# Sliding-window attention in slots: scores ahead of outputs and transposed probabilities, outputs a slot later, three probability buffers

## Chip, cores and metric

The kernel runs on one core of one Trainium2 chip. The metric is the device time of one execution in microseconds (us). The engines are named as in the profile: PE is the TensorE matrix engine, PEld its weight loads, DVE the VectorE, ACT the ScalarE, SP the engine that issues the DMAs here.

## The reference

The block has 1024 positions of width 1024. One input projection gives the operands of two branches: a gated linear attention (branch A) and sliding-window attention (branch B). Their gated sum goes through an output projection, and then a SwiGLU layer follows. Only branch B's attention is touched. Its heads: eight query heads of 128, two key/value heads (groups g = 0, 1, four query heads each). What it computes, for one query block of 128 positions and the up to three key blocks around it:

```
q, k = rms_norm(q) * q_g, rms_norm(k) * k_g        # then rotary positions
s = (q @ k^T) / sqrt(128), outside +-128: masked
p = softmax over [s, sink logit of the head]       # the sink has no value
o = p @ v
```

## The kernel before, in words

All matrices are float32, split in a high and a low half (names ending in h and l), and a product is three matmuls (`mm3`: high by high, high by low, low by high).

The section runs 16 tiles, numbered n = 8 g + t for group g and query block t, in 22 slots. In a slot, `slot` calls a list of stages; behind each stage it gives an equal share of the slot's n dense matmuls, the **fills** (`fill`): 128x512 matmuls of the projection of branch A's output gate, which depend on nothing in the attention. A slot has 26 fills for the first two slots, 15 up to slot 18 and 18 afterwards. So PE has fills to do between the stages, but runs all in the order in which the program writes it (`manual_schedule`): when a stage's matmul waits, the fills behind it wait. The order on DVE, ACT and SP is chosen when the program is built, by when operands are expected; each engine runs its list in that order.

The stages of tile n (in brackets the slot before the change):

- `k_load` and `a_load` (n - 1, n): DMA loads of value (kvr), key and query rows (qr).
- `k_prep` (n): value halves vSh (ACT), vSl (DVE). `a_prep` (n + 1): square on ACT (into sq4), sum on DVE (L867), normalising factor rs, and rotary products on DVE (L912, L914, L916, L917, result qn).
- `k_turn` (n + 1): keys transposed on PE (L900) into a `ch` tile, copied in halves to kTh, kTl. `a_turn` (n + 2): four query heads transposed (L923), copied to sqh (ACT L926) and sql (DVE L927).
- `a_scores` (n + 3), one stage per head: `mm3` into a `ch` tile, its mask addition and maximum in one DVE instruction (L941, writes p and mx). After the fourth head: mx, nm, es on DVE (L948 to L952), four exponentials on ACT with their sums (L956), dn and rd on DVE (L958, L960), four scalings of p on ACT (L962).
- `a_probs` (n + 5), one stage per key block: p transposed for four heads (L973) into a `ch` tile, copied to ph (ACT L976) and pl (DVE L977).
- `a_out` (n + 5): up to nine matmuls of ph, pl with vSh, vSl into a `ch` tile, a copy sob (ACT L987), four DMAs (L989).

All `ch` tiles come from one pool (psc, line 38) of four PSUM tiles, so a stage that wants a new one waits until the last reader of a tile's earlier content has run. Four more PSUM tiles (psm) belong to the fills; their results leave through DVE (L125) and a `stg` tile to DRAM. Weights of the fills are split on ACT (L70, wh) and DVE (L72, wl).

Within a slot the stages are sorted by the tuple `order`. The slots' contents are in the table `todo`. At t = 19 the pool of the small left-side tiles is closed, and `prep_b(0)` starts loading attention outputs back (lo, L1009), each split in obh (ACT L1001) and obl (DVE L1002), for the projection `branch_b(0)`, which follows the last slot and the remaining fills. Loads into lo have two buffers; their memory is that of pools that were just closed.

Of the kernel before, what the change touches and what calls it, by code (L numbers as in the profile page):

```python
# [8 lines left out]
F32 = mybir.dt.float32  # L9
# [5 lines left out]
P = 128  # L15
# [15 lines left out]
def body(tc, i, out):  # L31
    nc = tc.nc
    with ExitStack() as root:
# [8 lines left out]
        def nm(s):  # L42
            uid[0] += 1
            return f"{s}_{uid[0]}"
# [4 lines left out]
        def chtile(shape, dt=F32):  # L49
            return psc.tile(list(shape), dt, tag="ch", name=nm("ch"))  # L50
# [27 lines left out]
        def mm3(o, ah, al, bh, bl, start, stop):  # L78
            mm(o, ah, bh, start, False)
            mm(o, ah, bl, False, False)  # L80
            mm(o, al, bh, False, stop)
# [26 lines left out]
        stgs = ExitStack()  # L108
# [502 lines left out]
        stg = glas.enter_context(tc.tile_pool(name="stgA", bufs=4))  # L611
# [208 lines left out]
        with tc.manual_schedule(engines={mybir.EngineType.PE}):  # L820
            fill(24)
            for t in range(last + 1):
                n = 24 if t < 2 else 16 if t < 4 else 12 if t < NH * NC + 4 else 8 if t < last - 1 else 18
# [9 lines left out]

        sc_ = swas.enter_context(tc.tile_pool(name="swc", bufs=1))
        swe = swas.enter_context(tc.tile_pool(name="swe", bufs=2))
        stg = stgs.enter_context(tc.tile_pool(name="stg", bufs=4, side="right"))
        swl = stgs.enter_context(tc.tile_pool(name="swl", bufs=2, side="right"))
        swm = stgs.enter_context(tc.tile_pool(name="swm", bufs=1, side="right"))

        class sw:  # L840
            def tile(shape, dt, tag, name, bufs=2):
                pool = swm if tag in ("p", "ph", "pl") else swe if tag in (
                    "kvr", "key", "sq4", "qn4", "qr", "qh", "ql") else swl
                return pool.tile(shape, dt, tag=tag, name=name, bufs=bufs)
        cosb = load_const(sc_, "cosb", i["c_cos"], (P, KT, 64))
        sinb = load_const(sc_, "sinb", i["c_sin"], (P, KT, 64))
# [17 lines left out]
        def inv_norm(raw, n, sq, scale, epsv, eps_t):  # L864
            ss = sw.tile([P, n], F32, tag=f"ss{n}", name=nm("ss"))
            nc.scalar.activation(sq, raw[:, 0:n], AF.Square)
            nc.vector.tensor_reduce(ss, sq, axis=mybir.AxisListType.X, op=ALU.add)  # L867
            rs = sw.tile([P, n], F32, tag=f"rs{n}", name=nm("rs"), bufs=4)
            rsqrt(rs, ss, scale, epsv, eps_t, sw, (P, n), f"sn{n}")
            return rs  # L870
# [9 lines left out]
        def k_load(t):  # L880
            raws[t] = sw.tile([P, 256], F32, tag="kvr", name=nm("kvr"))
            need(("skv", t))
            nc.sync.dma_start(out=raws[t], in_=scr["skv", t][:, 256:512])
            keys[t] = sw.tile([P, 2, P], F32, tag="key", name=nm("key"))
            nc.sync.dma_start(out=keys[t].rearrange("p a b -> p (a b)"), in_=scr["key", t])
# [19 lines left out]
        def a_prep(g, n):  # L905
            a = att[g, n] = Chunk()
            qr = raws.pop((g, n))

            b = sw.tile([P, 4, P], F32, tag="sq4", name=nm("sq"))
            a.rs = inv_norm(qr, 4, b, 1.0, EPS * 128, eps128)  # L910
            a.qn = sw.tile([P, 4, P], F32, tag="qn4", name=nm("qn"))
            nc.vector.tensor_tensor(b[:, :, 0:64], qr[:, :, 64:128], qB[:, n:n + 1, 0:64].to_broadcast([P, 4, 64]),  # L912
                                    op=ALU.mult)
            nc.vector.tensor_tensor(b[:, :, 64:128], qr[:, :, 0:64], qB[:, n:n + 1, 64:128].to_broadcast([P, 4, 64]),  # L914
                                    op=ALU.mult)
            nc.vector.tensor_tensor(a.qn, qr, qA[:, n:n + 1].to_broadcast([P, 4, P]), op=ALU.mult)  # L916
            nc.vector.tensor_tensor(a.qn, a.qn, b, op=ALU.add)  # L917
# [13 lines left out]
        def a_scores(g, n, h):  # L931
            a = att[g, n]
            if h == 0:
                a.p = sw.tile([P, 4, 384], F32, tag="p", name=nm("p"))
                a.mx = sw.tile([P, 4], F32, tag="mx", name=nm("mx"))
            w, p, mx = a.w, a.p, a.mx
            ks = slice(a.b0 * P, (a.b1 + 1) * P)
            mo = (a.b0 - (n - 1)) * P
            s = chtile((P, 384))
            mm3(s[:, :w], a.qh[:, h], a.ql[:, h], kTh[:, g, ks], kTl[:, g, ks], True, True)  # L940
            nc.vector.tensor_tensor_reduce(out=p[:, h, :w], in0=s[:, :w], in1=band[:, mo:mo + w],  # L941
                                           op0=ALU.add, op1=ALU.max, scale=1.0, scalar=-1e30,
                                           accum_out=mx[:, h:h + 1])
            if h < 3:
                return
            sk = sink[:, 4 * g:4 * g + 4]
            nm_ = sw.tile([P, 4], F32, tag="nm", name=nm("nm"))
            nc.vector.tensor_tensor(mx, mx, a.rs, op=ALU.mult)  # L948
            nc.vector.tensor_tensor(mx, mx, sk, op=ALU.max)
            nc.vector.tensor_scalar(nm_, mx, -1.0, None, op0=ALU.mult)  # L950
            es = sw.tile([P, 4], F32, tag="es", name=nm("es"))
            nc.vector.tensor_tensor(es, sk, mx, op=ALU.subtract)  # L952
            nc.scalar.activation(es, es, AF.Exp)
            dn = sw.tile([P, 4], F32, tag="dn", name=nm("dn"))
            for h in range(4):
                nc.scalar.activation(p[:, h, :w], p[:, h, :w], AF.Exp, bias=nm_[:, h:h + 1],  # L956
                                     scale=a.rs[:, h:h + 1], accum_out=dn[:, h:h + 1])
            nc.vector.tensor_tensor(dn, dn, es, op=ALU.add)  # L958
            rd = sw.tile([P, 4], F32, tag="rd", name=nm("rd"))
            nc.vector.reciprocal(rd, dn)  # L960
            for h in range(4):
                nc.scalar.activation(p[:, h, :w], p[:, h, :w], AF.Copy, scale=rd[:, h:h + 1])  # L962
# [32 lines left out]
        oa, ob, mh, ml = {}, {}, {}, {}  # L995
# [16 lines left out]
        todo = [[] for _ in range(2 * KT + 6)]  # L1012
        for n in range(2 * KT):
            g, t = divmod(n, KT)
            todo[n + 5].append((a_out, g, t))
            todo[n + 5] += [(a_probs, g, t, kb) for kb in range(3)]
            todo[n + 3] += [(a_scores, g, t, h) for h in range(4)]
            todo[n + 2].append((a_turn, g, t))
            todo[n + 1].append((a_prep, g, t))
            if n < KT:  # L1020
                todo[n + 1].append((k_turn, n))
                todo[n].append((k_prep, n))
                if n:
                    todo[n - 1].append((k_load, n))
            todo[n].append((a_load, g, t))
        order = (a_probs, k_prep, a_prep, a_scores, a_turn, k_turn, a_out, k_load, a_load)
        k_load(0)
        with tc.manual_schedule(engines={mybir.EngineType.PE}):
            for t, v in enumerate(todo):
# [507 lines left out]
```

## Time and profile before

| | us |
|---|---|
| median of 3 runs | 1649.15 (1649.06 to 1649.78) |
| profiled execution | 1649.93 |
| its span | 1648.1 |
| PE busy in the span | 1628.2 (99%) |
| DVE, ACT busy | 1249.4 (76%), 872.3 (53%) |
| the attention slots | about 566 to 745 |

The span runs from the first to the last recorded instruction; 1.8 us of the profiled execution lie around it. In rows of the profile, "out<-in" names tiles, "L941" is a line of the program, and a bracket such as [0.48 <-DVE mx L941] is idle time of the engine just before the row and what released it. Matmuls are pipelined: a row of 0.39 us can be followed by the next matmul 0.23 us after its start.

### The profile page before, as it was taken

How to read it: one execution, taken by the hardware profiler on the slowest of the kernel's cores; microseconds unless marked ns; L12 is line 12 of the kernel's file. 1: busy time of each engine (PE TensorE's matmuls, PEld its weight loads, DVE VectorE, ACT ScalarE, POOL GpSimd, SP SyncE). 2: the span in 40 equal slices, each digit the busy share in tenths (PEclk: the TensorE clock that was granted, in tenths of full speed). 3: DMA queues.
4: the chain of work that ended last, by engine and by line, in shares of the span. 5: the costliest groups of instructions: out<-in, count | busy, mean ns of one | idle time of the engine just before them, and what ended most of it. 6: DMA issues, size and time to landing. Idle time of an engine off the chain costs nothing.

```text
span 1648.1 us, 23225 instructions
## 1 busy us (share of the span) xinstructions
PE 1628.2 (99%) x7588; PEld 1346.5 (82%) x7588; DVE 1249.4 (76%) x2559; ACT 872.3 (53%) x1826; POOL 0.2 (0%) x4
## 2 busy tenths in 40 slices
PE   9999999999999999999999999999999999999999
PEld 7888888888888778878888888888888888888887
DVE  8867665589986599857885678887777778779655
ACT  8622224468998688885554557333333333354442
POOL 0000000000000000000000000000000000000000
PEclk9999999999999999999999999999999999999999
DMA  7554334485554633238765554453334443496433
GB/s 235 171 184 147 116 118 138 170 253 173 178 162 128 190 115 97 74 124 280 226 205 171 168 152 148 128 160 109 103 109 155 146 147 128 168 349 192 147 98 120
DMA packets 168010, 262.90 MB, mean 160 GB/s; under 512 B 19325, under 2 KB 52861, under 8 KB 167889
## 3 DMA queue, kind: packets, MB, share of 16 engines
q1 hardware_dynamic: 167888, 261.42, 49.9%
q8 instruction: 60, 0.98, 0.3%
q14 instruction: 62, 0.50, 0.1%
HBM read 187.93 MB, written 73.42 MB: 159 GB/s over the span
## 4 chain that ended last, share of the span: by engine, by line
PE 84%; DVE 8%; ACT 5%; DMA 1%; issue 1%; SPq 0%; ACTq 0%
PE mm L76 23%; PE mm L306 9%; PE mm L308 9%; PE mm L307 9%; PE mm L1350 7%; PE ch L1350 5%; PE ch L76 4%; PE ch L308 4%; PE ch L307 4%; PE ch L306 4%; PE ch L460 3%; PE mm L460 2%; ACT p L956 1%; DVE cs L655 1%; DVE wl L72 1%
## 5 line engine op out<-in xcount | busy, mean ns | idle before, releaser
L298 ACT ACTIVATE wh<-ws 128x512 fp32r<-128x512 f32 x132 | 83.3, 632 | 196.6 <-PE mm L307 104.5
L70 ACT ACTIVATE wh<-wr 128x512 fp32r<-128x512 f32 x202 | 124.9, 626 | 83.3 <-PE mm L76 47.7
L72 DVE TENSOR_TENSOR wl<-wr,wh 128x512 fp32r<-128x512 f32 x202 | 137.2, 684 | 26.3 <-ACT wh L70 26.1
L298 ACT ACTIVATE wh<-wr 128x512 fp32r<-128x512 f32 x69 | 43.6, 632 | 125.0 <-issue 49.9
L299 DVE TENSOR_TENSOR wl<-ws,wh 128x512 fp32r<-128x512 f32 x132 | 90.2, 684 | 22.4 <-ACT wh L298 22.3
L298 ACT ACTIVATE wh<-a 128x512 fp32r<-128x512 f32 x64 | 40.5, 633 | 91.1 <-PE mm L1350 42.6
L76 PE MATMUL mm<-wh,xl 128*128 128x512 f32 x192 | 83.0, 432 | 0.0
L76 PE MATMUL mm<-wh,xh 128*128 128x512 f32 x192 | 79.7, 415 | 0.0
L76 PE MATMUL mm<-wl,xh 128*128 128x512 f32 x192 | 79.6, 414 | 0.0
L299 DVE TENSOR_TENSOR wl<-a,wh 128x512 fp32r<-128x512 f32 x64 | 44.2, 690 | 43.0 <-ACT wh L298 42.6
L1350 PE MATMUL mm<-hh,wh 128*128 128x512 f32 x176 | 68.5, 389 | 0.0
L1350 PE MATMUL mm<-hl,wh 128*128 128x512 f32 x176 | 68.5, 389 | 0.0
L1350 PE MATMUL mm<-hh,wl 128*128 128x512 f32 x176 | 68.5, 389 | 0.0
L76 PE MATMUL mm<-xh,wh 128*128 128x512 f32 x160 | 64.6, 404 | 1.2 <-ACT wh L70 1.2
L76 PE MATMUL mm<-xl,wh 128*128 128x512 f32 x160 | 64.5, 403 | 0.1
L76 PE MATMUL mm<-xh,wl 128*128 128x512 f32 x160 | 59.2, 409 | 0.0
L1320 DVE TENSOR_TENSOR hl<-hr,hh 128x512 fp32r<-128x512 f32 x75 | 51.3, 684 | 3.7 <-ACT hh L1319 3.7
L1350 PE MATMUL ch<-hh,wh 128*128 128x512 f32 x132 | 51.3, 389 | 0.0
L1350 PE MATMUL ch<-hl,wh 128*128 128x512 f32 x132 | 51.3, 389 | 0.0
L1350 PE MATMUL ch<-hh,wl 128*128 128x512 f32 x132 | 51.3, 389 | 0.0
L76 PE MATMUL mm<-oah,wh 128*128 128x512 f32 x128 | 50.2, 392 | 0.0
L76 PE MATMUL mm<-oal,wh 128*128 128x512 f32 x128 | 49.8, 389 | 0.0
(620 smaller groups left out, 5058.6 us busy)
## 6 DMA issues: line engine op xcount, KB each, us to landing
wr<-in_w_fi_dram SPq DMA_DIRECT2D x102, 256.0 KB
wr<-in_w_f_dram SPq DMA_DIRECT2D x80, 256.0 KB
wr<-in_w_t_dram SPq DMA_DIRECT2D x56, 256.0 KB
B<-c SPq DMA_DIRECT2D x44, 256.0 KB
T<-tx SPq DMA_DIRECT2D x44, 256.0 KB
a<-in_w_fo_dram SPq DMA_DIRECT2D x44, 256.0 KB
hr<-T SPq DMA_DIRECT2D x44, 256.0 KB
wr<-in_w_ob_dram SPq DMA_DIRECT2D x32, 256.0 KB
```

Of the source, the lines that this page charges most:

```text
L70: nc.scalar.activation(h, raw, AF.Copy)
L72: nc.vector.tensor_tensor(l, raw, h.bitcast(F32), op=ALU.subtract)
L76: nc.tensor.matmul(o, a, b, start=start, stop=stop)
L298: nc.scalar.activation(h, src, AF.Copy)
L299: nc.vector.tensor_tensor(l, src, h.bitcast(F32), op=ALU.subtract)
L306: nc.tensor.matmul(o, h[:, c], x[kk][0], start=start and kk == 0, stop=False, skip_group_check=True)
L307: nc.tensor.matmul(o, h[:, c], x[kk][1], start=False, stop=False, skip_group_check=True)
L308: nc.tensor.matmul(o, l[:, c], x[kk][0], start=False, stop=kk == nk - 1, skip_group_check=True)
L460: nc.tensor.matmul(ys[m], a[:, c], b, start=f0, stop=f1, skip_group_check=True)
L655: nc.vector.tensor_tensor_scan(csf, mask.rearrange("p c t -> p (c t)"), ef, 0.0, op0=ALU.mult, op1=ALU.add)
L1320: nc.vector.tensor_tensor(l, r, h.bitcast(F32), op=ALU.subtract)
L1350: nc.tensor.matmul(ys[m], a[:, c], b, start=f0, stop=f1, skip_group_check=True)
```

## The change

Line numbers after line 842 are one lower in the changed program (L941 becomes L940).

```
-        stg = stgs.enter_context(tc.tile_pool(name="stg", bufs=4, side="right"))
+        stg = stgs.enter_context(tc.tile_pool(name="stg", bufs=3, side="right"))
...
-                pool = swm if tag in ("p", "ph", "pl") else swe if tag in (
-                    "kvr", "key", "sq4", "qn4", "qr", "qh", "ql") else swl
+                pool = swm if tag in ("p", "ph", "pl") else swl if tag == "ob" else swe
...
-            b = sw.tile([P, 4, P], F32, tag="sq4", name=nm("sq"))
+            b = sw.tile([P, 4, P], F32, tag="sq4", name=nm("sq"), bufs=1)
...
-                a.p = sw.tile([P, 4, 384], F32, tag="p", name=nm("p"))
+                a.p = sw.tile([P, 4, 384], F32, tag="p", name=nm("p"), bufs=3)
...
-            todo[n + 5].append((a_out, g, t))
+            todo[n + 6].append((a_out, g, t))
...
-        order = (a_probs, k_prep, a_prep, a_scores, a_turn, k_turn, a_out, k_load, a_load)
+        order = (a_scores, a_out, a_turn, k_turn, k_prep, a_prep, a_probs, k_load, a_load)
```

The probabilities p get a third buffer (two were the default), sq4 one instead of two, the stg tiles of the fills three instead of four, and the small tiles move from the pool swl on the right side of the memory to swe on the left, which is closed at t = 19. In a slot, the scores of tile n come first, then the output of tile n - 3 (whose probabilities were transposed a slot before), then the transposes of queries and keys, the preparations, and the transposed probabilities of tile n - 2 at the end.

In PE's order this is written out by the two lines above. On the other engines the new order follows from it; three places.

On DVE, early in the section: the reductions of the third tile's scores (mx_7210 before, mx_7171 after; ch is the score's tile, st a result of the fills, wl a weight half, sq and qn belong to a_prep, dn and rd to the tile before). Before:

```order
L916 TENSOR_TENSOR qn_7186<-qr_7166,qA 128x512
L912 TENSOR_TENSOR sq_7173<-qr_7166,qB 128x4x64
L125 TENSOR_TENSOR st_7193<-mm_6983,rstd 128x512
L917 TENSOR_TENSOR qn_7186<-qn_7186,sq_7173 128x512
L958 TENSOR_TENSOR dn_7130<-dn_7130,es_7127 128x4
L125 TENSOR_TENSOR st_7197<-mm_6984,rstd 128x512
L960 RECIPROCAL rd_7136<-dn_7130 128x4
L72 TENSOR_TENSOR wl_7206<-wr_7202,wh_7204 128x512
L941 ISA p_7209,mx_7210<-ch_7211,band 128x384
L941 ISA p_7209,mx_7210<-ch_7217,band 128x384
```

After:

```order
L72 TENSOR_TENSOR wl_7198<-wr_7194,wh_7196 128x512
L940 ISA p_7170,mx_7171<-ch_7172,band 128x384
L125 TENSOR_TENSOR st_7185<-mm_6983,rstd 128x512
L940 ISA p_7170,mx_7171<-ch_7178,band 128x384
L957 TENSOR_TENSOR dn_7107<-dn_7107,es_7104 128x4
L125 TENSOR_TENSOR st_7189<-mm_6984,rstd 128x512
L959 RECIPROCAL rd_7113<-dn_7107 128x4
L940 ISA p_7170,mx_7171<-ch_7201,band 128x384
L940 ISA p_7170,mx_7171<-ch_7207,band 128x384
L915 TENSOR_TENSOR qn_7266<-qr_7166,qA 128x512
```

The two stores' products st and dn, rd stood ahead of the first reduction and now stand among the reductions; a_prep's products of the tile that was loaded last (qr_7166) stood ahead of the reductions and now stand behind all four.

On DVE, late in the steady slots, around one sql (the low half of a turned query, wanted by the next slot's first score). Before:

```order
L941 ISA p_8676,mx_8677<-ch_8703,band 128x384
L927 TENSOR_TENSOR sql_8734<-ch_8728,sqh_8733 128x512
L916 TENSOR_TENSOR qn_8804<-qr_8756,qA 128x512
L917 TENSOR_TENSOR qn_8804<-qn_8804,sq_8791 128x512
L72 TENSOR_TENSOR wl_9061<-wr_9057,wh_9059 128x512
L958 TENSOR_TENSOR dn_8715<-dn_8715,es_8712 128x4
L960 RECIPROCAL rd_8721<-dn_8715 128x4
L941 ISA p_8811,mx_8812<-ch_8813,band 128x384
```

After:

```order
L916 TENSOR_TENSOR qn_8703<-qn_8703,sq_8690 128x512
L957 TENSOR_TENSOR dn_8643<-dn_8643,es_8640 128x4
L959 RECIPROCAL rd_8649<-dn_8643 128x4
L926 TENSOR_TENSOR sql_8685<-ch_8679,sqh_8684 128x512
L940 ISA p_8744,mx_8745<-ch_8746,band 128x384
L976 TENSOR_TENSOR pl_8715<-ch_8709,ph_8714 128x512
```

Before, dn (which waits for the exponentials on ACT) stood between sql and the next slot's first reduction; here it now stands ahead of sql. In other slots of the changed program sql stays ahead of dn.

On ACT, at the end of the section, from the last tile's exponentials on (p_9042 before, p_8994 after; obh are the halves of the loads lo, ph the transposed probabilities, sob the copies of outputs). Before:

```order
L956 ACTIVATE p_9042,dn_9083<-p_9042,nm_9076,rs_8795 128x256 x4
L1001 ACTIVATE obh_9128<-lo_9126 128x512
L962 ACTIVATE p_9042<-p_9042,rd_9089 128x256 x4
L1001 ACTIVATE obh_9134<-lo_9132 128x512
L976 ACTIVATE ph_9179<-ch_9174 128x512
L976 ACTIVATE ph_9192<-ch_9187 128x512
L976 ACTIVATE ph_9206<-ch_9201 128x512
L1001 ACTIVATE obh_9140<-lo_9138 128x512
```

After:

```order
L986 COPY sob_9052<-ch_9042 128x512
L961 ACTIVATE p_8994<-p_8994,rd_9034 128x256 x4
L975 ACTIVATE ph_9071<-ch_9066 128x512
L975 ACTIVATE ph_9082<-ch_9077 128x512
L975 ACTIVATE ph_9093<-ch_9088 128x512
L1000 ACTIVATE obh_9112<-lo_9110 128x512
L986 COPY sob_9168<-ch_9158 128x512
L1000 ACTIVATE obh_9118<-lo_9116 128x512
L975 ACTIVATE ph_9183<-ch_9178 128x512
```

Before, two obh stood ahead of the ph that the same slot's output needs. Now the ph of the next tile to be put out stand ahead of the first obh, and two obh and a sob stand ahead of the ph of the tile behind it.

## The prediction

> **What bounds the kernel now.** I read the page's totals first, then the waits of TensorE (PE), then stretches of the section that the diff touches (568 to 740 us), then single rows in time. Totals:
>
> ```profile
> PE 1628.2 (99%) x7588; PEld 1346.5 (82%) x7588; DVE 1249.4 (76%) x2559; ACT 872.3 (53%) x1826; POOL 0.2 (0%) x4
> ```
>
> PE is busy nearly throughout, and the change takes no matmul away: only gaps in the PE stream can be won. The waits of PE that fall in this section (waited for, us in total, times, longest):
>
> ```profile
> PE ch L76 <- DVE mx L941: 3.1, 6, 0.7
> PE ch L923 <- DVE mx L941: 2.0, 2, 1.8
> PE ch L76 <- ACT ph L976: 2.0, 1, 2.0
> PE ch L76 <- DVE rd L960: 1.1, 2, 0.7
> PE ch L923 <- DVE qn L917: 1.0, 1, 1.0
> PE ch L76 <- DVE pl L977: 0.9, 1, 0.9
> PE ch L923 <- DVE rt L102: 0.5, 1, 0.5
> ```
>
> Together 10.6 us. Where they lie, by stretches (width, then busy time of PE, PEld, DVE, ACT, POOL; granted clock, DMA):
>
> ```profile
> 568.00:610.00 42.00, 37.84 (x201) 30.91 (x200) 40.84 (x137) 32.97 (x89) 0.00 (x0) 1.00 0.44 131
> 610.00:720.00 110.00, 105.54 (x579) 89.03 (x578) 92.69 (x310) 93.20 (x239) 0.00 (x0) 1.00 0.28 88
> 720.00:730.00 10.00, 9.86 (x55) 7.49 (x53) 4.84 (x18) 7.41 (x20) 0.00 (x0) 1.00 0.40 133
> 730.00:740.00 10.00, 7.96 (x32) 5.78 (x30) 5.66 (x11) 9.37 (x19) 0.00 (x0) 0.83 0.65 209
> ```
>
> PE idles 4.16 us in the ramp (slots 1 to 4, DVE busy 40.84 of 42), 4.46 in the steady slots, 0.14 and 2.04 at the end. A stall costs more than its idle time, as the rows of the tail show:
>
> ```profile
> 732.12 0.40 PE L76 MATMUL mm<-xh,wh 128*128 128x512 f32 x1
> 732.36 0.39 PE L76 MATMUL mm<-xl,wh 128*128 128x512 f32 x1
> 734.72 0.78 PE L76 MATMUL ch<-ph,vSh 128*128 128x512 f32 x1 [1.97 <-ACT ph L976]
> 735.56 0.80 PE L76 MATMUL ch<-pl,vSh 128*128 128x512 f32 x1
> ...
> 738.25 0.40 PE L76 MATMUL ch<-pl,vSh 128*128 128x512 f32 x1
> ```
>
> Matmuls start 0.24 apart (0.23 over longer stretches) while a row lasts 0.39, so each stall loses its idle and 0.16 more: here 734.72 - 732.36 - 0.23 = 2.13. Then the clock falls (0.83 in this stretch): the next start comes 0.61 late, and the six steps from 735.56 to 738.25 take 2.69 instead of 1.38, 1.31 more. The tail loses 2.13 + 0.61 + 1.31 = 4.05 us. With 0.16 for each of some 7 stalls the ramp loses 5.3, with some 10 the steady part 6.0, the last slot 0.3: **15.7 us** in all, 0.95% of the time, is the most that the change can win.
>
> **A steady stall**, on PE, DVE and ACT:
>
> ```profile
> 691.62 0.39 PE L76 MATMUL mm<-xh,wh 128*128 128x512 f32 x1
> 692.49 0.44 PE L76 MATMUL ch<-kTh,sqh 128*128 128x384 f32 x1 [0.48 <-DVE mx L941]
> 691.60 0.17 DVE L958 TENSOR_TENSOR dn<-dn,es 128x4 f32<-128x4 f32 x1 [2.25 <-ACT p L956]
> 691.90 0.53 DVE L941 CUSTOM_DVE_ANT_0 p<-ch,band 128x384 f32<-128x384 f32 x1
> 688.12 0.59 ACT L987 COPY sob<-ch 128x512 f32<-128x512 f32 x1 [1.86 <-PE ch L76]
> 688.71 0.70 ACT L956 ACTIVATE p<-p,nm,rs 128x384 f32<-128x384 f32 x1
> 690.78 0.69 ACT L956 ACTIVATE p<-p,nm,rs 128x384 f32<-128x384 f32 x1
> ```
>
> Three transposed probabilities hold three of the four `ch` tiles, so the second score takes the tile of the first and waits for its reduction (L941). That stands on DVE behind dn, dn behind four exponentials on ACT, those behind the copy sob, and that behind the output matmuls. One fill between the scores leaves 0.64 us lost.
>
> **The change part by part.**
>
> Buffers. The wait views have no row in which a reduction waits for a p buffer, a load for sq4, or stg for its store. The third p is needed since scores now run before the transposes of the tile two back; by itself it saves nothing. sq4 with one buffer makes the next square (ACT) wait for DVE's a_prep of the tile before, a slot earlier; stg with three has one projection's two stores every 27 us or so. Both nothing, bounds -0.3 to +1. Stores of outputs come a slot later on SP's queue, four issues each; the first reader is prep_b, priced in the tail.
>
> The ramp. The longest stall, and DVE ahead of it:
>
> ```profile
> 590.01 0.66 PE L923 MATMUL ch<-ident,qn 128*128 128x128 f32 x4 [1.81 <-DVE mx L941]
> 585.13 0.68 DVE L916 TENSOR_TENSOR qn<-qr,qA 128x512 f32<-128x512 f32 x1
> 587.99 0.68 DVE L125 TENSOR_TENSOR st<-mm,rstd 128x512 f32<-128x512 f32 x1
> 589.40 0.55 DVE L941 CUSTOM_DVE_ANT_0 p<-ch,band 128x384 f32<-128x384 f32 x1
> ```
>
> The a_prep work, two L125, a wl and dn precede the first reduction; in the changed order two reductions precede dn and both L125, and a_prep follows all four. Some 4 us of DVE work leave the queue ahead, so the 1.81 + 0.16 = 2.0 goes. What comes next is the same work, due a slot later at the next qt: DVE idles only 42 - 40.84 = 1.2 us in the ramp, and of its work only three pl (1.8) are put off past it, so the ramp cannot win over 3.0. Some of the small stalls go too (0.3).
>
> Against it stands the start:
>
> ```profile
> 563.18 0.43 SPq L883 DMA_DIRECT2D kvr<-skv  x1
> 563.66 0.43 SPq L885 DMA_DIRECT2D key<-key  x1
> 567.20 0.42 ACT L894 ACTIVATE vSh<-kvr 128x256 fp32r<-128x256 f32 x1 [4.17 <-DMA kvr<-skv]
> 568.10 0.38 PE L900 MATMUL ch<-ident,key 128*128 128x128 f32 x2
> 573.52 0.68 DVE L917 TENSOR_TENSOR qn<-qn,sq 128x512 f32<-128x512 f32 x1
> 574.26 0.66 PE L923 MATMUL ch<-ident,qn 128*128 128x128 f32 x4 [0.96 <-DVE qn L917]
> ```
>
> kt is now the first stage of slot 1, ten fills (2.3 us) earlier, at 565.8, when its key is still under way (kvr, issued 0.48 before it, was waited for until 567.2): about 1.6 us of stall. The first qt comes five fills (1.1 us) earlier while qn still ends at 574.2. The two overlap, since PE waits for the same end of qn: up to there 0.96 becomes about 2.1, 1.1 more. Ramp: -2.0 - 0.3 + 1.1 = **-1.2** (bounds -3.0 and +1).
>
> The steady slots. The output is now a slot behind its transposes and follows the scores, so it no longer waits for pl, and rotation changes which tile each score gets: in the built program 8 scores before and 6 now take the tile of the score just ahead. Two fewer by 0.64 to 0.8 is -1.4; against it, second scores that take the tile of a transpose and so wait for its pl: 5 slots, 3 before; between nothing and the 0.9 that the one wait for pl took, I take 0.25 each, near nothing since only some of it shows as idle, +0.5. **-0.9**. Bounds: -3 (half the steady loss), +4 (below, the second rival in part of the slots).
>
> The tail. Chain on ACT ahead of the long wait:
>
> ```profile
> 730.92 0.62 ACT L1001 ACTIVATE obh<-lo 128x512 fp32r<-128x512 f32 x1
> 731.96 1.71 ACT L962 ACTIVATE p<-p,rd 128x256 f32<-128x256 f32 x4 [0.42 <-DVE rd L960]
> 733.57 0.61 ACT L1001 ACTIVATE obh<-lo 128x512 fp32r<-128x512 f32 x1
> 734.09 1.54 ACT L976 ACTIVATE ph<-ch 128x512 fp32r<-128x512 f32 x3
> 732.48 0.33 SPq L1009 DMA_DIRECT2D lo<-b  x1
> 735.66 0.63 ACT L1001 ACTIVATE obh<-lo 128x512 fp32r<-128x512 f32 x1
> ```
>
> The output of a slot needed a ph of the same slot, behind exps, scales and two obh. Now it needs the slot before's. From the last score the first such output finds: nm 0.9, four exps 2.4, sob 0.5, scales 1.7, ph 0.5, pl 0.6, 6.6 us; PE gets there after an output (2.1), three transposes (1.1) and some eleven fills (2.5), 5.7: about 0.9 lost. The next output wants the second ph, behind an obh whose lo can only be issued after the first obl and a store; lo took 3.2 us (732.48 to 735.66). Worked on from the same score: the first lo lands 3.2 after the scales (9.0), obh and sob to 10.2, third lo issued and landed at 13.8, obh and ph to 15.0, pl 15.6; PE gets there after the lost 0.9, outputs, transposes and fills at 14.9: about 0.5. No idle near 2 us, so I count no fall of the clock. 1.4 instead of 4.05: **-2.6** (bounds -4 and +1, a longer wait with the slow clock again). In the last slot -0.2.
>
> [...]
>
> Sum: -1.2 - 0.9 - 0.2 - 2.6 = **-4.9**. From the profiled execution's 1649.93 (span 1648.1 and 1.8 around it) that is 1645.0; this execution stands 0.8 over the median 1649.15, so I forecast **1644.2**.
>
> **The rivals.** 0.2% is 3.3 us, about what a measurement can tell from no change.
>
> First, the steady stalls stay: there are still four `ch` tiles, and the steady wait is for one of them. For it: the row of 692.49, and the reductions of the six remaining scores. Then -0.9 becomes +0.5 and, with a tail of 2.5 to 3, the sum is -2.0: **1647**. [...] A form of this rival is that the change does not do what it says: the scheduler places the same waits elsewhere.
>
> Second, **slower**: the first score of a slot waits for sql. In five of the later slots DVE has dn and rd ahead of sql, and dn waits for exps that stand behind sob, which now waits for an output placed right behind the scores. Price from rows: output 9 x 0.23 and a fill, 2.5 after the last score's start; sob 0.6; exps 2.9; dn, rd 0.3; sql 0.6: 6.9. The matmul that needs sql comes after 12 fills, an output, qt, three transposes and 0.35: about 6.85. It is just hidden; an ACT late by more than that pays it in every slot. The rest loses 5.7, so from 10.0 / 14 = 0.71 us a slot the change is a loss; at 1.05 it is 14.7 + 5.7 - 15.7 = +4.7: **1653.9**. Against it: only a part of the slots has this order.
>
> **How the numbers follow.** Forecast (a gain over 3.3) 0.51; the first rival, and a ramp or a tail that gives less than counted, 0.31; the second, with a tail that falls back, 0.18. Range: below, ramp and tail at -3.0 and -3.5 with -2 between, 1640.5; above, most of the second rival, 1653. About 0.05 lies below and 0.15 above. The likeliest case's own range is 1640.5 to 1645.9.
>
> **What would show it.** Right: no PE wait near 2 us for mx in the ramp, a new one for the key or qn before 575, PEclk 1.00 through the tail, steady idle near 3.7. Wrong: PE waits for sql (L926 after) in each slot, or ph behind obh with the clock below 1 again.

## The result, and the profile after

The changed kernel takes 1655.64 us (median of 6 runs, 1653.38 to 1656.64) against 1649.18 (1649.06 to 1649.78): ratio 1.0036, interval [1.0026, 1.0046]. It is **slower by 0.36%**, 6.5 us; the forecast was 5 us faster, and the time lies above the range. The profiled execution has a span of 1654.0 us, 5.9 more than before. The stretches that the prediction used, in the changed kernel (width, then busy time of PE, PEld, DVE, ACT, POOL; granted clock, DMA):

```profile
568.00:610.00 42.00, 40.32 (x216) 33.83 (x215) 41.48 (x143) 35.83 (x96) 0.00 (x0) 1.00 0.43 131
610.00:720.00 110.00, 100.87 (x536) 83.13 (x535) 88.05 (x295) 88.19 (x226) 0.00 (x0) 0.98 0.26 82
720.00:730.00 10.00, 7.75 (x37) 6.19 (x36) 4.92 (x18) 5.76 (x13) 0.00 (x0) 0.83 0.09 27
730.00:740.00 10.00, 9.06 (x47) 7.00 (x46) 4.20 (x10) 8.09 (x21) 0.00 (x0) 1.00 0.75 237
```

PE's idle time fell in the ramp (1.68 instead of 4.16, though one wait now lies just ahead of 568), doubled in the steady slots (9.13 instead of 4.46), appeared in the last one (2.25 instead of 0.14) and fell in the tail (0.94 instead of 2.04). The clock of 0.83 stands a slot earlier. What PE waits for:

```profile
PE ch L76 <- DVE sql L926: 5.9, 6, 2.2
PE ch L76 <- DVE mx L940: 2.7, 7, 0.4
PE ch L972 <- DVE sql L926: 1.7, 1, 1.7
PE ch L899 <- DMA qr<-sq: 1.6, 1, 1.6
PE ch L76 <- DVE pl L976: 1.3, 2, 1.1
PE ch L76 <- DVE kTl L902: 1.1, 2, 0.7
PE ch L76 <- ACT ph L975: 0.7, 1, 0.7
PE ch L76 <- DVE rs L104: 0.6, 1, 0.6
```

No wait of PE named sql before; now it is the largest, 7.6 us in seven waits. mx is down from 5.1 to 2.7. (L899 transposes the key; its row names another load, qr, as what ended the wait.) The largest of the new waits, on PE, then on DVE and on ACT:

```profile
715.21 0.34 PE L76 MATMUL ch<-kTh,sqh 128*128 128x384 f32 x1
...
718.51 0.60 PE L922 MATMUL ch<-ident,qn 128*128 128x128 f32 x4
...
721.83 0.40 PE L76 MATMUL mm<-xl,wh 128*128 128x512 f32 x1
724.48 0.39 PE L76 MATMUL ch<-kTh,sqh 128*128 128x256 f32 x1 [2.25 <-DVE sql L926]
```

```profile
717.40 0.17 DVE L949 TENSOR_SCALAR nm<-mx 128x4 f32<-128x4 f32 x1
...
720.61 0.16 DVE L957 TENSOR_TENSOR dn<-dn,es 128x4 f32<-128x4 f32 x1 [2.98 <-ACT p L955]
720.81 0.18 DVE L959 RECIPROCAL rd<-dn 128x4 f32<-128x4 f32 x1
723.73 0.69 DVE L926 TENSOR_TENSOR sql<-ch,sqh 128x512 fp32r<-128x512 f32 x1 [2.74 <-ACT sqh L925]
```

```profile
717.61 0.71 ACT L955 ACTIVATE p<-p,nm,rs 128x384 f32<-128x384 f32 x1 [2.32 <-DVE nm L949]
...
720.49 0.56 ACT L986 COPY sob<-ch 128x512 f32<-128x512 f32 x1
721.08 2.13 ACT L961 ACTIVATE p<-p,rd 128x384 f32<-128x384 f32 x4
723.12 0.57 ACT L925 ACTIVATE sqh<-ch 128x512 fp32r<-128x512 f32 x1
```

The turned query is ready on PE at 719.1, and its copy sqh needs 0.57 us, but ACT's list has the exponentials, sob and four scalings ahead of it. DVE's list has dn and rd ahead of sql, but they end at 720.99, and then DVE stands idle for 2.74 us until sqh is there. sql ends 9.2 us after the last score started (715.21); PE wanted it after 6.9 (722.06).

The matmul that waits at 724.48 reads kTh and sqh, which both come from ACT. The one that reads sql is the third of the score and starts at 724.82. So PE waits here not for an operand but for the `ch` tile: the score takes the tile of the turned query, whose last reader is sql. All six waits for sql at a score stand at such a first matmul. The seventh stands at a transpose of probabilities, which never reads sql:

```profile
628.34 0.63 PE L972 MATMUL ch<-ident,p 128*128 128x128 f32 x4 [1.66 <-DVE sql L926]
```

Over the section, the copy sqh stands behind the exponentials of the same slot on ACT for seven of the 16 tiles. It starts 2.3 to 4.0 us after its transposes end there. These seven are the ones for which PE waits; for the other nine the profile has no wait for sqh or sql. In six of the seven sql starts 0.03 us after sqh has ended, so DVE's list adds nothing; in the seventh it adds 0.36 us, behind two products for stores and rd.

Measured from start to start of the matmuls (a start later than its usual distance counts as lost), the parts lose, in us:

| part | before | forecast | after |
|---|---|---|---|
| ramp, with the first key | 5.3 | 4.1 | 4.1 |
| steady slots | 6.0 | 5.1 | 12.8 |
| last slot of scores | 0.3 | 0.1 | 3.4 |
| tail | 4.05 | 1.4 | 1.55 |

The parts sum to 6.2 us more than before. From PE's matmul 2700 to its matmul 3800, which enclose the section, the changed execution takes 233.8 us instead of 226.5, so about 1 us more is lost than this count finds. It reaches matmul 2700 1.4 us earlier than the execution before, for a reason that no run shows.

### The profile page after: what moved, and what is told of

The parts are those of the page before. It is cut to its first block, busy times and chain, and to the rows that moved or that the text cites. A ratio compares the mean times of both kernels' runs of the same rounds, so it can differ in the third digit from the quotient of the medians.

```text
span 1654.0 us, 23233 instructions
## 1 busy us (share of the span) xinstructions
PE 1630.2 (99%) x7588; PEld 1347.8 (81%) x7588; DVE 1249.3 (76%) x2559; ACT 873.3 (53%) x1826; POOL 0.2 (0%) x4
## 4 chain that ended last, share of the span: by engine, by line
PE 86%; DVE 7%; ACT 5%; DMA 1%; issue 1%; SPq 0%; ACTq 0%
PE mm L76 24%; PE mm L306 9%; PE mm L307 9%; PE mm L308 9%; PE mm L1349 7%; PE ch L1349 5%; PE ch L76 5%; PE ch L306 4%; PE ch L308 4%; PE ch L307 4%; PE ch L460 3%; PE mm L460 2%; ACT p L955 1%; DVE wl L72 1%; DVE cs L655 1%
```

## The experiments

My theory after the result: the time lost is the wait of the first score of a slot for sql, whose making is queued on ACT behind the exponentials (and what precedes and follows them) and on DVE behind dn. Rivals: the buffers (one sq4, three stg) delay the chain; the four `ch` tiles make scores at the head of a slot slow by themselves; outputs a slot later put sob ahead of the exponentials, and that alone is the loss. All ratios are to runs of the kernel before on the same chip, whose medians were 1649.15 to 1649.61. The changed kernel was timed once, beside 1649.18, and differences from it are of medians.

**Buffers and pools alone.** The change with these two lines as before:

```
-        order = (a_scores, a_out, a_turn, k_turn, k_prep, a_prep, a_probs, k_load, a_load)
+        order = (a_probs, k_prep, a_prep, a_scores, a_turn, k_turn, a_out, k_load, a_load)
-            todo[n + 6].append((a_out, g, t))
+            todo[n + 5].append((a_out, g, t))
```

> The buffers and pools of the change alone: p three, sq4 one, stg three, small tiles on the left; order of stages and slot of the outputs as before. Theory (the added time is the wait of a slot's first score for sql, whose chain on DVE and ACT stands behind the exponentials): the order of before keeps sql ahead of dn, so the time is that of before, 1649 to 1650, and no PE wait for sql over 0.3 us. Rival (one sq4 buffer and three stg tiles make ACT and DVE wait for each other, and that is what delays the chain): 1652 or more, with ACT waiting for the sum in a_prep as in the changed kernel.

Measured: 1646.37 us, ratio 0.9984 [0.9975, 0.9994], faster than the kernel before. No wait for sql; the buffers are not the cause. Neither theory nor rival expected the gain: the steady part is as before, the tail is not (below).

**Turns before outputs.** The changed kernel with

```
-        order = (a_scores, a_out, a_turn, k_turn, k_prep, a_prep, a_probs, k_load, a_load)
+        order = (a_scores, a_turn, k_turn, a_out, k_prep, a_prep, a_probs, k_load, a_load)
```

> The changed kernel with the stages of a slot in the order scores, turns, outputs, preparations, transposed probabilities (turns and outputs swapped, nothing else). Theory: sqh and sql now stand ahead of the exponentials and of dn on their engines; the PE waits for sql (5.9 + 1.7 us and the slow clock after them) go, the steady part loses about 6 us instead of 16, and the time is 1644 to 1648. Rival (the four PSUM tiles and scores at the head of the slot make the steady part slow by themselves): PE waits for mx and pl take the place of those for sql, 1652 to 1656.

Measured: 1647.91 us, ratio 0.9995 [0.9985, 1.0004], 7.7 us under the changed kernel by this one swap. PE's waits, and the steady stretch and the next:

```profile
PE ch L76 <- DVE mx L940: 3.8, 9, 0.6
PE ch L76 <- DVE pl L976: 1.8, 3, 1.0
PE ch L76 <- ACT ph L975: 1.7, 1, 1.7
PE ch L899 <- DMA kvr<-skv: 1.3, 1, 1.3
```

```profile
610.00:720.00 110.00, 105.11 (x573) 87.55 (x573) 91.62 (x309) 94.19 (x237) 0.00 (x0) 1.00 0.28 85
720.00:730.00 10.00, 8.07 (x34) 6.03 (x33) 4.18 (x11) 6.79 (x18) 0.00 (x0) 0.84 0.77 229
```

All waits for sql are gone, and the steady stretch idles 4.89 us, about the 4.46 of the kernel before. sqh stands ahead of the exponentials for all 16 tiles. Scores still stand at the head of the slot and the tiles are still four, so these two do not make the loss by themselves. But the swap can also give the first score another tile, so this run alone does not tell a late sql from an unlucky tile; the runs with dn and with sob, which leave PE's order as changed, help there. Scores first buys nothing in the steady part either. The tail (ph, 1.7, clock 0.84) is as long as before, although the outputs come a slot later.

**Turns at the head of the slot.**

```
-        order = (a_scores, a_out, a_turn, k_turn, k_prep, a_prep, a_probs, k_load, a_load)
+        order = (a_turn, k_turn, a_scores, a_out, k_prep, a_prep, a_probs, k_load, a_load)
```

> The changed kernel with the turns at the head of the slot: turns, scores, outputs, preparations, transposed probabilities. A query is then turned a whole slot before its first score. Theory: no PE wait for sql at all, 1643 to 1648, with the start of the section a little worse (the first qt comes earlier than its qn). Rival (scores at the head of the slot are the cause): 1652 to 1656, since the scores still precede outputs and probabilities.

Measured: 1665.54 us, ratio 1.0101 [1.0086, 1.0116]; a miss. The largest waits:

```profile
PE ch L76 <- DVE pl L976: 9.3, 12, 2.0
PE ch L922 <- DVE qn L916: 4.0, 3, 2.5
PE ch L76 <- DVE mx L940: 3.0, 7, 0.9
```

sql is gone, as expected, but a query's and three probabilities' transposes now hold all four `ch` tiles when the scores come, and the first scores wait for the pl that reads one of them. In this kernel's order of DVE the pl stand behind dn and rd as sql did. Removing one waiter from behind dn put another there.

**Outputs later, old order.** The changed kernel with

```
-        order = (a_scores, a_out, a_turn, k_turn, k_prep, a_prep, a_probs, k_load, a_load)
+        order = (a_out, a_probs, k_prep, a_prep, a_scores, a_turn, k_turn, k_load, a_load)
```

> The old order of stages with the outputs a slot later, at the head of the slot: outputs, probabilities, preparations, scores, turns; buffers as changed. Theory: in all slots sql stands ahead of dn, so no wait for sql; the tail loses 1.5 instead of 4, the ramp keeps its long wait for mx; 1645 to 1649. Rival (outputs a slot later make sob stand ahead of the exponentials, and that alone delays everything behind): PE waits longer for mx, 1652 or more.

Measured: 1651.17 us, ratio 1.0010 [1.0000, 1.0019], 4.5 us under the changed kernel, between the range of the theory and that of the rival. No wait for sql. It is 4.8 us slower than the buffers alone (1646.37, timed beside it): waits for sob (1.5 us, 5 times) and slightly more for mx (3.7 us, 11 times, instead of 3.5, 8 times) come with it. So with the outputs at the head of the old order, putting them a slot later costs about half of the 9.3 us that lie between the buffers alone and the changed kernel. With turns before outputs, where they also come a slot later, only 1.5 us lie between.

**dn off VectorE.** The changed kernel with

```
-            nc.vector.tensor_tensor(dn, dn, es, op=ALU.add)
+            nc.gpsimd.tensor_tensor(dn, dn, es, op=ALU.add)
-            nc.vector.reciprocal(rd, dn)
+            nc.scalar.activation(rd, dn, AF.Ln)
+            nc.scalar.activation(rd, rd, AF.Exp, scale=-1.0)
```

> The changed kernel with the sum dn on GpSimd and the reciprocal on ACT (exp of minus log), so that no DVE instruction waits for the exponentials; PE's order unchanged. Theory (dn, queued ahead of sql on DVE and waiting for ACT, is what delays sql): PE waits for sql fall from 7.6 us to under 2 and the time to 1645 to 1650, though ACT has 0.6 us a slot more. Rival (sqh, queued on ACT behind the exponentials, delays sql by itself): the waits stay above 4 us and the time at 1651 to 1656.

Measured: 1651.02 us, ratio 1.0009 [1.0000, 1.0018], 4.6 us under the changed kernel in spite of more work on ACT (busy 96.22 us in 610 to 720, against 94.19 with turns before outputs). What is left of the sql wait:

```profile
PE ch L76 <- DVE sql L926: 2.0, 3, 1.1
...
PE ch L76 <- ACT sqh L925: 0.9, 2, 0.5
```

2.9 us for both halves instead of 7.6, between the theory's "under 2" and the rival's "above 4"; the time is just inside the rival's range. The order on ACT was chosen anew too, so the sum does not tell which queue did it, but single tiles do. For tiles n = 13 and 14 ACT's list has sqh behind the exponentials in both kernels. The first score of n = 14, in the changed kernel and in this one:

```profile
712.38 0.44 PE L76 MATMUL ch<-kTh,sqh 128*128 128x384 f32 x1 [1.21 <-DVE sql L926]
709.61 0.44 PE L76 MATMUL ch<-kTh,sqh 128*128 128x384 f32 x1 [1.15 <-DVE sql L926]
```

For n = 13 the wait is 0.67 us there and 0.68 here. With dn gone from DVE nothing changed for these two, so dn ahead of sql is not what delays sql. The waits went for n = 6, 7 and 9, whose sqh now stands ahead of the exponentials on ACT, and for n = 8, whose exponentials no longer stand behind sob. For n = 15, whose sqh now stands ahead of the scalings, the wait fell from 2.25 to 0.21 us. The two waits for sqh are new, for n = 10 and 11, where it now stands behind the exponentials. So single tiles speak against the theory of this run and for its rival, sqh queued behind the exponentials.

**sob on VectorE.** The changed kernel with

```
-            nc.scalar.copy(ob, o)
+            nc.vector.tensor_copy(ob, o)
```

> The changed kernel with the copy sob of the outputs on DVE instead of ACT; all else as changed. Theory (the exponentials start late because sob, which waits for an output placed right behind the scores, precedes them on ACT): exponentials start 0.5 to 1 us sooner after nm, the chain to sql ends before PE needs it in most slots, 1646 to 1650. Rival (sob does not matter, the chain is long by its exponentials alone): waits for sql as before, 1653 to 1658 with 0.6 us more work a slot on DVE.

Measured: 1651.26 us, ratio 1.0010 [1.0000, 1.0019], 4.4 us under the changed kernel, just outside the 1646 to 1650 expected. PE has no wait for sql, but not for the reason expected. Of the seven tiles in question, the exponentials start sooner after the last score in two (0.6 us), at the same time in one and 0.7 to 1.1 us later in four. What changed is ACT's list, which has sqh behind the exponentials for two tiles instead of seven. For the last of these two neither sob nor the scalings stand between, and sql ends 6.6 us after the last score's start instead of 9.2, just in time. With sob on DVE, which is busy 98.64 us in 610 to 720 against 91.62 with turns before outputs, the wait for pl is 5.0 us (6 times) instead of the changed kernel's 1.3. ACT's own waits in 610 to 730, of the changed kernel and of this one:

```profile
ACT rl L98 <- DVE ss L866: 12.9, 7, 2.6
ACT sob L986 <- PE ch L76: 6.0, 9, 1.6
```

```profile
ACT rl L98 <- DVE ss L866: 11.4, 8, 2.7
ACT sqh L925 <- PE ch L922: 6.5, 7, 1.8
```

The changed kernel's longest wait on ACT, for the sum ss of a_prep, looks like a suspect. It is almost as long here, where sql is in time, so it is not the cause; sqh now waits for PE and not PE for it.

**The pool line alone**, in the kernel before:

```
-                pool = swm if tag in ("p", "ph", "pl") else swe if tag in (
-                    "kvr", "key", "sq4", "qn4", "qr", "qh", "ql") else swl
+                pool = swm if tag in ("p", "ph", "pl") else swl if tag == "ob" else swe
```

> The kernel before with one line of the change: small tiles on the left side, closed at slot 19 (p two, sq4 two, stg four, old order). Theory: the loads lo wait longer for their memory, so obh is queued on ACT behind the transposed probabilities and not ahead of them; the tail loses 1 us instead of 4, PEclk 1.00 in 730 to 740, 1646 to 1647.5, all of the gain that buffers and pools together gave. Rival (the gain came from the buffer counts): tail as before, 1648.5 to 1650.

Measured: 1647.52 us, ratio 0.9986 [0.9977, 0.9996]. ACT and PE's stretch in the tail:

```profile
730.51 0.58 ACT L975 ACTIVATE ph<-ch 128x512 fp32r<-128x512 f32 x1
731.11 1.71 ACT L961 ACTIVATE p<-p,rd 128x256 f32<-128x256 f32 x4
732.73 1.05 ACT L975 ACTIVATE ph<-ch 128x512 fp32r<-128x512 f32 x2
735.55 0.59 ACT L986 COPY sob<-ch 128x512 f32<-128x512 f32 x1 [1.77 <-PE ch L76]
736.03 1.15 ACT L1000 ACTIVATE obh<-lo 128x512 fp32r<-128x512 f32 x2
```

```profile
730.00:740.00 10.00, 9.45 (x47) 7.24 (x46) 6.08 (x12) 7.00 (x16) 0.00 (x0) 1.00 0.68 202
```

The first loads lo are issued later, in the kernel before (first row) and here:

```profile
725.43 0.80 SPq L1009 DMA_DIRECT2D lo<-b  x2
732.85 0.80 SPq L1008 DMA_DIRECT2D lo<-b  x2
```

So their halves obh come later and are queued behind the ph. By the program, the loads take memory of the pools closed at t = 19, which now hold small tiles that the last scores still use; that this is what holds the loads back is argued from the program and not shown. The tail idles 0.55 instead of 2.04 us with the clock at 1.00. By the start of PE's matmul 3600 this execution is 3.4 us ahead of the one before (0.3 at the section's start); by the medians the gain is 2.0 us. The gain of the tail is this line's, with outputs in their old slot.

**Scores first in the ramp only.** Buffers alone, as above, with the new order in slots 3 and 4:

```
-                v.sort(key=lambda e: order.index(e[0]))
+                v.sort(key=lambda e: (late if t in (3, 4) else order).index(e[0]))
```

where `late` is the new order.

> Buffers and pools of the change, old order and old slot of the outputs, but in slots 3 and 4 alone the new order of stages. Theory: the long wait for mx in the ramp (2.3 us lost at 589) goes, without the wait for the key at the start; steady part and tail as with the buffers alone: 1643.5 to 1645.5, faster than both kernels. Rival (DVE is full in the ramp, so the work put off is only waited for later): 1646 to 1647, as with the buffers alone, with a new wait before 610.

Measured: 1646.65 us, ratio 0.9982 [0.9973, 0.9992]; as the buffers alone, and a miss. The 2.2 us wait at 589 is gone, and in the ramp waits of 1.2 us for pl (at 594.75), 0.7 for rs, 0.6 for kTl and smaller ones stand in its place; PE still idles 3.7 us there, instead of 4.4 with the buffers alone. DVE is busy 40.97 of 42 us: putting the scores first mostly chooses who waits for it.

**Fills given out differently**, with turns before outputs and with the old order:

```
-  26 if t < 2 else 15 if t < 2 * KT + 3 else 18
+  34 if t < 1 else 26 if t < 2 else 15 if t < 2 * KT + 2 else 27 if t < 2 * KT + 3 else 18
```

> Turns before outputs as in the run of that name, and fills given out differently: slot 0 has 34 instead of 26, slot 18 has 27 instead of 15 (they come from those left over after the last slot). Theory (what that run still loses at the ends is PE arriving early, at the first key and at the transposed probabilities of the tail): the first wait (1.3 us) and the long one of the tail with its slow clock (4.2 lost) go, the steady waits for mx and pl stay, 1642 to 1645, faster than both kernels. Rival (the tail is bound by the chain of ACT whatever PE does before): 1646 to 1648.

Measured: 1646.6 us, ratio 0.9983 [0.9973, 0.9993]. The waits at the first key and in the tail went (in the tail 0.2 us for a pl is the longest left, PEclk 1.00), so the rival's reason is wrong though the time lies in its range; a wait of 1.9 us for kTh at 599 came. Faster than both kernels, by less than expected.

```
-  26 if t < 2 else 15 if t < 2 * KT + 3 else 18
+  26 if t < 2 else 24 if t < 5 else 15 if t < 2 * KT + 3 else 18
```

> Buffers and pools of the change, old order, and 24 fills instead of 15 in slots 2 to 4. Theory (in the ramp DVE is full, so only work of PE that needs no DVE hides the wait): the 2.2 us wait for mx before 590 and the small ones after it go, 3 to 4 us, 1642.5 to 1644. Rival (the waits only move to later slots, as when the scores were put first there): 1646 to 1647.

Measured: 1650.96 us, ratio 1.0010 [1.0001, 1.0020]; a miss, with the theory's first half right. The ramp's waits vanish:

```profile
568.00:610.00 42.00, 41.37 (x220) 35.03 (x219) 41.01 (x136) 32.15 (x85) 0.00 (x0) 1.00 0.48 150
610.00:720.00 110.00, 104.92 (x568) 87.30 (x567) 91.75 (x307) 92.51 (x234) 0.00 (x0) 1.00 0.26 81
...
740.00:760.00 20.00, 16.29 (x60) 11.35 (x59) 12.73 (x20) 11.10 (x18) 0.00 (x0) 0.88 0.77 242
```

but 3.71 us of idle with a slow clock (0.88) stand after 740, where the projection starts before its obh and obl are there (PE waits 3.0 us for obh, 0.7 for obl). The fills that slots 2 to 4 now use were left over for after the last slot, and would have lain there.

## Why the prediction was wrong, point by point

**What bounds the kernel**: right. PE's stream is the time, and the gaps in it account for the result.

**The ramp, -1.2**: right in size and kind (4.1 lost, as forecast). The 1.81 us wait for mx is gone, and a new 1.6 us wait for the key stands in the list. The key and the first qn together were counted as 2.1 us; the wait for the first qn went altogether. The run with scores first in two slots, and the one with more fills there, speak for DVE's load and not the order as what sets the rest.

**The steady slots, -0.9, and the last slot, -0.2**: this is the step that failed. They came to +6.8 and +3. The working looked at the tiles that second scores take, where it was about right: the steady waits for mx and rd fell from 3.6 to 1.9 us. There it did not look at what the first score of a slot needs: the turned query, and in these slots that query's `ch` tile. The chain to sql was worked out only in the second rival, as 6.9 us against a need at 6.85, and taken as hidden. In the seven tiles with a wait it took 7.1 to 9.2. The sum has dn and rd between the exponentials and sql; the runs show sqh there, 0.6 us, which the sum counted as free on ACT. In six of the seven the list reads exponentials, sqh. In the last slot exponentials end 5.3 after the last score's start, earlier than the 6.0 of that sum, but then sob (which the sum had ahead of them) and four scalings (which it left out), 2.6 together, come before sqh.

That sqh's place on ACT is the cause is shown from two sides: the seven late tiles are the seven waits, and sob off ACT, with PE's order unchanged, took the waits away by the lists it led to. The run with dn off DVE shows that dn is not: where sqh kept its place, the waits stayed. The swap of turns and outputs, which brings 7.7 us, fits but also changes the tiles. What stays open is the part of the four tiles. Waiting for the tile, PE stops at the first matmul of a score instead of the third, some 0.3 us sooner (724.48 and 724.82 above), and the wait at 628.34 is for a tile alone; no run has another number of tiles. No edit moved sqh on ACT and nothing else, either.

**The second rival, 0.18**: it was the outcome and the place, and half of the mechanism: the wait for sql behind the exponentials is there, but through sqh on ACT and not through dn on DVE. Its size is luck. It put 14.7 us on 14 slots and 1653.9; steady and last slot lost 16.2 and the median is 1655.6, but seven tiles waited, 7.6 us in all, and the rest are other waits and the slow clock (0.57 from 643 to 647, 0.83 in 720 to 730). Its chance was too low because "just hidden" rested on two sums that agreed within 0.05 us, while the chains measured differ by 2 us from tile to tile.

**The tail, -2.6**: the size came out (1.55 against 1.4 lost), and so did the chain: exponentials, sob, scalings and ph on ACT, the ph ending 7.0 us after the last score's start where 6.0 was counted, and PE there at 6.4 where 5.7 was counted. That the outputs a slot later win it did not come out. The pool line alone, with outputs in their old slot, ends the long wait too. With turns before outputs, where they come a slot later, the same exponentials start 0.9 us later and PE waits 1.7 us with the clock at 0.84. So that the change got the forecast size is partly luck.

**The buffers, nothing**: wrong by the tail's gain of the line that moves small tiles, 2 us by the medians and 3 in the profiled executions; sq4 with one buffer and stg with three cost nothing that the runs show.

Of the signs named for being wrong, "PE waits for sql in each slot" came true for seven tiles of 16, and the clock was below 1 again, in the last slot of scores (0.83) and not in the tail (1.00).

## What to carry to other kernels

When stages are reordered and each engine runs its list in order, as here (behind the wait of 1.66 us at 628.34 stood two fills, which need nothing of the attention), follow every operand of the first stage of the new slot, and the last reader of the buffer that it takes, back through each engine's list, and add all that stands ahead there, not only the chain of data. When an instruction is late, see whether its engine was busy or idle just before it: in the slot shown DVE was idle for 2.74 us, waiting for ACT, and dn ahead of sql cost nothing. Two sums that meet within a few hundredths mean an even chance, not cover. A line that only moves buffers between pools came here with the next phase's first loads at 732.85 instead of 725.43 and a gain of 2.0 us: run such a line alone before crediting the reorder.

## What the runs showed of the hardware

The granted clock fell (0.57 from 643 to 647) where no single wait was long. PE in the changed kernel, after three short waits:

```profile
640.73 0.39 PE L76 MATMUL ch<-kTh,sqh 128*128 128x256 f32 x1 [0.67 <-DVE sql L926]
...
641.88 0.39 PE L76 MATMUL ch<-kTh,sqh 128*128 128x256 f32 x1 [0.29 <-DVE mx L940]
...
643.03 0.44 PE L76 MATMUL ch<-kTh,sqh 128*128 128x256 f32 x1 [0.29 <-DVE mx L940]
...
645.62 0.63 PE L76 MATMUL ch<-ph,vSh 128*128 128x512 f32 x1
646.05 0.63 PE L76 MATMUL ch<-pl,vSh 128*128 128x512 f32 x1
```

A 128x512 matmul starts 0.43 after the one before it here instead of 0.23, and its row lasts 0.63 instead of 0.39; the granted clock from 643.3 to 646.8 is 0.52. A wait of 1.66 us at 628.34 in the same kernel, followed by one of 0.74 at 630.41, brought no such stretch (clock 1.00 from 627 to 637), nor did 1.81 us at 590.01 in the kernel before (1.00 from 588 to 594). The three waits above were 1.25 us together; 2.25 us at 724.48 in the same kernel and 1.97 us at 734.72 in the kernel before stand in stretches with 0.83. So in these runs the length of a wait alone does not tell whether the clock falls, and the prediction's step from no idle near 2 us to no fall of the clock does not hold. What else decides it, no run shows.
